# A macaron encoder trunk on one core: three more chunks' down products by seven, a fourth raw buffer, sums into x as two-block views, operands from x times norm weights

## The chip, the cores and the metric

One core of one Trainium2 chip runs the whole program. The time is device microseconds from launch to end. Of the kernel before there are three runs: 2550.9, 2551.19 and 2552.08 us, median 2551.19. One more execution was profiled; its span is 2552.6 us.

In the profile, PE is the matrix engine (PEld its weight loads, which run beside the matmuls), DVE is VectorE, ACT is ScalarE, POOL is GpSimd, and SP is the engine whose queue issues the loads. L12 is line 12 of the kernel.

## What is computed

Two layers, each of a half-step feed-forward block, a mixer (gated short convolution and band attention), and a second half-step feed-forward block; then a final norm. There are 640 token columns (512 of a prompt and 8 x 16 of samples), 1024 channels and 2816 hidden features. All is in float32.

```
def _rmsnorm(x, g):
    xf = x.astype(jnp.float32)
    y = xf * lax.rsqrt(jnp.mean(xf * xf, axis=-1, keepdims=True) + EPS)
    return y.astype(x.dtype) * g

def _swiglu(h, w_gu, w_down):
    gu = h @ w_gu
    g, u = jnp.split(gu, 2, axis=-1)
    return (jax.nn.silu(g) * u) @ w_down

for l in range(DEPTH):
    xp = xp + 0.5 * _swiglu(_rmsnorm(xp, norm_ffn1[l]), w_ffn1_gu[l], w_ffn1_down[l])
    mp, cnp, knp, vnp = _mixer(_rmsnorm(xp, norm_mix[l]), ...)
    xp = xp + mp
    xp = xp + 0.5 * _swiglu(_rmsnorm(xp, norm_ffn2[l]), w_ffn2_gu[l], w_ffn2_down[l])
```

The same runs for the samples, xs. The matter here is the feed-forward blocks, called a0 and b0 in the first layer, a1 and b1 in the second.

## The kernel before

The state x stays in SBUF, transposed: eight tiles x[k] of 128 channels by 640 columns. Columns are halved: t1 is the first 320, t2 the second, and each half of a result has a PSUM bank of its own.

**Precision in three products.** Each float32 operand is split into a high part (a cast on ScalarE, ACT.copy) and a low part (the difference, on VectorE). A product is three matmuls: high by high, high by low, low by high. For weights this is `prep` (L283 and on): the cast whi at L296, and the low split wlo, queued in `pending` and put out by `flush` at L301. Split weights (slabs) have three buffers each.

**Weights.** All weights lie in DRAM as one stream of [128, 1024] blocks in the order of use. `kinds` lists the blocks' kinds; `load` fetches the next block into a raw buffer, of which there are three, through SP's queue. A buffer is free again when the last split of what it held has read it.

**By seven.** Gate and up of one hidden part of 128 features are computed together as a 2 x 2 block product with seven multiplications instead of eight. Two blocks of weights (ra, rb) make four slabs: ra as it is, a sum s65 (two additions at L240, the first of which reads rb), ra after two more additions, and half of rb. `gate_up` runs the seven products, 12 matmuls each, in the order X11, X21, N6, T5, T7, X22, T4, in PSUM banks pa, pb and pc. A product that goes on in pa (N6, T7, T4) follows a read of pa: by ScalarE (c1, u2) or by VectorE (g from pa and c5, before T4).

**Down products.** The 22 hidden parts of a block are cut into chunks (`FFNS`: the chunks' sizes, and how many parts the opening of a0 computes in another way). While the gate and up products of one chunk run, the down products of the chunk before are mixed in. `by_seven` says which chunks have down products by seven as well: chunks of four parts, not those of the opening, and not the last. For those, `Pair` builds the seven operands of two hidden parts (sums on VectorE, a cast on ScalarE, a low split on VectorE, at places that `TURNS` names), and `down_rows` is called twice in the next chunk, after its second and third part (`ROWS`): each call makes four of the eight rows of x. Its seven products, again 12 matmuls each, run in two-bank tiles A and B and two single banks c. What it adds to x is taken from PSUM in three ways: by VectorE directly (`take`, L980), or copied to SBUF by ScalarE (`stage`, L967 and L970) and added by an accumulating DMA that POOL issues (`send`, L975). For other chunks, a down product is one sum over the chunk's parts in a two-bank tile and one update of x on VectorE (L1088).

**Norms.** The norm of the next block is applied after its products: VectorE and ScalarE build operands from x times the norm weights while the last chunk's down products run (`Expand.final`, L516; `norm` for the mixer), and a factor rho per column, found from the sum of squares, multiplies the results. Before the change, the operands of b0, a1 and b1 are multiplied by the previous norm's factor too (`self.prev.rr`), which rho then takes out again (`diagonal`, `inverse`).

**Order.** Within blocks named `manual_schedule(engines=ORDERED)`, PE, VectorE and ScalarE run in the order of the program. From the third part on after the first chunk by seven (`free` in `ffn`) only PE does; the other engines' order is chosen by the scheduler at build time. Every engine executes in order what it was given.

Of the kernel before, what the change touches and what calls it, by code (L numbers as in the profile page):

```python
# [16 lines left out]
P = 128  # L17
# [19 lines left out]
CH = 1024  # L37
# [7 lines left out]
FFNS = {"a0": ((4, 2, 4, 4, 4, 4), 4), "b0": ((2, 4, 4, 4, 8), 0),  # L45
        "a1": ((2, 4, 4, 4, 4, 4), 0), "b1": ((2, 4, 4, 4, 5, 3), 0)}
# [76 lines left out]
def kinds():  # L123


    out = []

    def plain(n):
        out.extend([8] * (n // 8) + [n % 8] * (n % 8 > 0))

    def ffn(name):
        held = 0
        for what, a in ffn_order(name):
            if what == "gu":
                plain(held)
                held = 0
                out.append("gu")
            elif what == "std":
                held += 2 * KT
            elif what == "cut":  # L140
                plain(held)
                held = 0
            elif what == "rows":
                plain(held)
                held = 0
                out.append("gu")
            else:
                held += sum(len(js) for _, js in a)
        plain(held)

    for l in range(L):
        ffn(f"a{l}")
        held = 0
        for what, _ in mixer_order():
            if what == "mix":
                plain(held)
                held = 0
                out.append("mix")
# [16 lines left out]
def trunk(ctx: ExitStack, tc: tile.TileContext, xin, wst, small, pbias, samplebias, kcache, vcache,  # L175
# [43 lines left out]
    slabs, n = [], 0  # L219
    for kind in kinds():  # L220
        if kind in ("gu", "mix"):
            slabs += [(kind, n, i) for i in range(4)]
            n += 2
        else:
            slabs.append(("plain", n, kind * P))
            n += 1
    assert n == wst.shape[0]
# [175 lines left out]
    x = [xp.tile([P, T], F32, name=f"x{k}") for k in range(KT)]  # L403
# [9 lines left out]
    def norm(name, goff, ssum):  # L413
# [18 lines left out]
        st.caps = sp.tile([P, T], F32, tag="rr", name=f"caps{name}", bufs=2)  # L432
        st.rr = sp.tile([P, T], F32, tag="rr", name=f"rr{name}", bufs=2)
# [45 lines left out]
    class Expand(Stats):  # L479
# [4 lines left out]
        def __init__(self, fp, name, goff, prev):  # L484
            super().__init__(name)
            self.fp, self.goff, self.prev = fp, goff, prev
# [3 lines left out]
            self.sq = self.rest = self.rr = None  # L490
            self.known = False

        def final(self, m, square=True):
# [19 lines left out]
            if self.prev is None:  # L513
                DVE.tensor_scalar(out=B, in0=halves(x[m]), scalar1=g, scalar2=None, op0=ALU.mult)
            else:
                DVE.scalar_tensor_tensor(out=B, in0=halves(x[m]), scalar=g, in1=halves(self.prev.rr),  # L516
                                         op0=ALU.mult, op1=ALU.mult)
# [80 lines left out]
        def inverse(self):  # L598

            self.rr = sp.tile([P, T], F32, tag="rr", name=f"rr{self.name}", bufs=2)  # L600
            DVE.tensor_tensor(out=self.rr, in0=self.rho, in1=self.prev.rr, op=ALU.mult)

    def opening(fp, name, goff, n, put, tails):
# [4 lines left out]
        ex = Expand(fp, name, goff, None)  # L608
# [22 lines left out]
        def out(i):  # L631
# [10 lines left out]
            u = tmp(f"u{name}_{j}") if j > 1 else sp.tile([P, T], F32, tag="rr", name=f"u{name}_{j}", bufs=2)  # L642
# [99 lines left out]
    def gate_up(fp, n, ex, first, turned, tails, put, j, pair, later, at):  # L742
# [127 lines left out]
        if first and turned:  # L870
            tails.append(ex.inverse)
# [65 lines left out]
    def down_rows(fp, n, ms, pairs, tails, later):  # L937
# [34 lines left out]

        def send(z, r, cols):
            for u in range(2):
                POOL.dma_start(x[ms[2 * u + r]][:, cols], z[:, u], accum_op=ALU.add)  # L975

        def take(ps, r, cols, scale=0.5):
            for u in range(2):
                xs = x[ms[2 * u + r]][:, cols]
                DVE.scalar_tensor_tensor(out=xs, in0=ps[u], scalar=scale, in1=xs, op0=ALU.mult, op1=ALU.add)  # L980
# [11 lines left out]
        take(b, 0, t1)  # L992
# [11 lines left out]
        send(stage("c7_", A, -0.5), 1, t2)  # L1004
# [9 lines left out]
        take(a, 1, t1, -0.5)  # L1014
        flush()

    def ffn(name, fp, ex, goff, after, end=False):
# [19 lines left out]
        for what, a in ffn_order(name):  # L1037
# [6 lines left out]
            if what == "gu":  # L1044
                turned = after is not None and not end
# [8 lines left out]
                gate_up(fp, f"{name}_{a}", ex, a == plain, turned, tails, act.__setitem__, a, pair, later,  # L1054
# [45 lines left out]
    def mixer(l, after):  # L1100
        with tc.tile_pool(name=f"yp{l}", bufs=1, reuse_waits="tile") as yp, \
# [3 lines left out]
            h, st, stats = norm(f"m{l}", O_GM + l * KT, yas[:, 0, :])  # L1105
# [85 lines left out]
        ex = after(st)  # L1191
# [444 lines left out]
    class Final:  # L1636
# [7 lines left out]
        def all(self, ops):  # L1644
            ws = [[tiles.take() for _ in ops] for m in range(KT)]
            flush()
            rr = sp.tile([P, PARTS[0].stop], F32, tag="rr", name="frr", bufs=2)
# [86 lines left out]
    for l in range(L):  # L1734
# [6 lines left out]
        def after(st):  # L1741
            open_pool(f"fp{l}")
            return Expand(pool[0], f"b{l}", O_G2 + l * KT, st)

        ex = mixer(l, after)
        if l < L - 1:
            ex = ffn(f"b{l}", pool[0], ex, 0,
                     lambda: Expand(pool[0], f"a{l + 1}", O_G1 + (l + 1) * KT, ex))
# [137 lines left out]
```

## Time and profile before

| what | value |
|---|---|
| median of three runs | 2551.19 us |
| span of the profiled execution | 2552.6 us |
| first layer: a0, mixer, b0 | to 440.7, to 853.4, to 1277.8 us |
| second layer: a1, mixer | to 1701.0, to 2113.7 us |
| second layer: b1 and the final norm | to 2552.6 us |
| TensorE's granted clock | 0.998 |
| bytes read from HBM | 225.85 MB |

How to read the profile's lines. A line of waits names the engine, tile and line that waited, after the arrow what ended the wait, and then the total in us, how often, and the longest. A line of the chain in order of time has a start, a duration and what ran; the chain is the work that ended last, followed back from the end. A line of a stretch has its bounds and length, then busy time and number of instructions of PE, PEld, DVE, ACT and POOL, the granted clock, the share of the DMA engines and GB/s. A line of a group has the code line, engine, operation, output and inputs, shapes and count, then busy time in us and the mean of one in ns, and after the second bar the idle time before it and what ended it. Matmuls overlap: one is shown with some 309 ns, but the next of 320 columns starts 147 ns later.

### The profile page before, as it was taken

What the parts mean: (1) busy time and instruction counts of PE and PEld (TensorE: products, weight loads), DVE (VectorE), ACT (ScalarE), POOL (GpSimd) and SP (SyncE); (2) the same over time, 40 slices, a digit from 0 to 9 for tenths busy, and PEclk for the clock granted to TensorE, in tenths of its full rate; (3) what the DMA queues carried; (4) which work ended last, traced back from release to release, by engine and by line L of the source; (5) the groups of instructions that cost most, each with busy time, mean ns of one, the idle gap of its engine ahead of it and who ended that gap; (6) DMA issues with size and microseconds to landing.
All of it is one profiled execution on the core that took longest, in us unless ns stands there. A gap on an engine that the chain in (4) does not pass through costs nothing.

```text
span 2552.6 us, 43143 instructions
## 1 busy us (share of the span) xinstructions
PE 2517.7 (99%) x17264; PEld 2452.2 (96%) x17264; DVE 2095.1 (82%) x3337; ACT 1290.9 (51%) x2036; POOL 243.9 (10%) x361
## 2 busy tenths in 40 slices
PE   8999999999999999999999999999999999999998
PEld 8999999888999999999999999998899999999998
DVE  7788988778677998988799888887786778988875
ACT  5345555665444545555445555556654445455543
POOL 0002111111000002111000122111110000022200
PEclk9999999999999999999999999999999999999999
DMA  3235454335222225443223555443442222255532
GB/s 134 67 102 124 114 127 115 113 104 169 75 85 87 73 96 124 111 117 104 83 83 102 122 124 124 109 109 122 128 136 83 75 91 79 87 124 124 123 101 75
DMA packets 104026, 271.19 MB, mean 106 GB/s; under 512 B 11568, under 2 KB 49072, under 8 KB 103824
## 3 DMA queue, kind: packets, MB, share of 16 engines
q1 hardware_dynamic: 70272, 223.90, 27.2%
q0 software_dynamic: 32832, 43.88, 10.1%
q8 instruction: 135, 2.21, 0.4%
q10 hardware_dynamic: 720, 0.65, 0.1%
q14 instruction: 67, 0.55, 0.1%
HBM read 225.85 MB, written 7.94 MB: 92 GB/s over the span
## 4 chain that ended last, share of the span: by engine, by line
PE 77%; DVE 13%; DMA 4%; ACT 3%; issue 2%; DVEq 0%; ACTq 0%
PE paa L386 10%; PE pab L386 8%; DVE wlo L301 5%; DMA raw<-in_wst 4%; PE py L363 4%; PE pdb L363 4%; PE po L363 4%; PE pda L363 4%; PE pca L386 4%; PE qa L386 4%; PE pcb L386 3%; PE daa L953 3%; PE pba L386 2%; PE pv L1392 2%; PE ma_cv L386 2%; PE dab L953 2%
## 5 line engine op out<-in xcount | busy, mean ns | idle before, releaser
L296 ACT CAST whi<-raw 128x1024 fp32r<-128x1024 f32 (+1 forms) x566 | 506.0, 898 | 390.7 <-PE pca L386 46.5
L301 DVE TENSOR_TENSOR wlo<-raw,whi 128x1024 fp32r<-128x1024 f32 (+1 forms) x566 | 581.5, 1031 | 120.3 <-ACT whi L296 116.6
L296 ACT CAST whi<-s 128x1024 fp32r<-128x1024 f32 (+1 forms) x146 | 137.9, 945 | 245.5 <-DVE s L240 107.6
L386 PE MATMUL pab<-xhib,whi 128*128 128x320 f32 x704 | 220.1, 313 | 9.0 <-DVE gb L240 8.3
L386 PE MATMUL pab<-xlob,whi 128*128 128x320 f32 x704 | 217.3, 309 | 0.0
L386 PE MATMUL pab<-xhib,wlo 128*128 128x320 f32 x704 | 217.3, 309 | 0.0
L386 PE MATMUL paa<-xhia,whi 128*128 128x320 f32 x640 | 199.7, 312 | 8.4 <-DVE ga L240 7.2
L386 PE MATMUL paa<-xloa,whi 128*128 128x320 f32 x640 | 197.5, 309 | 0.0
L386 PE MATMUL paa<-xhia,wlo 128*128 128x320 f32 x640 | 197.5, 309 | 0.0
L301 DVE TENSOR_TENSOR wlo<-s,whi 128x1024 fp32r<-128x1024 f32 (+1 forms) x146 | 158.8, 1088 | 13.8 <-ACT whi L296 13.8
L975 POOL DMA_DIRECT2D x<-c_b x72 | 65.4, 981 | 992.4 <-ACT whi L296 778.4
L240 DVE TENSOR_TENSOR s<-raw 128x512 f32<-128x512 f32 x110 | 75.7, 688 | 94.7 <-DMA raw<-in_wst 94.3
L975 POOL DMA_DIRECT2D x<-c_a x84 | 75.3, 961 | 799.7 <-ACT whi L296 589.6
L386 PEld LDWEIGHTS pab<-xhib,whi 128*128 128x128 f32 x704 | 132.1, 188 | 14.3 <-DVE gb L240 13.0
L386 PEld LDWEIGHTS paa<-xhia,whi 128*128 128x128 f32 x640 | 120.0, 188 | 13.0 <-DVE ga L240 11.6
L386 PEld LDWEIGHTS pab<-xlob,whi 128*128 128x128 f32 x704 | 132.1, 188 | 0.2
L386 PEld LDWEIGHTS pab<-xhib,wlo 128*128 128x128 f32 x704 | 132.1, 188 | 0.0
L386 PEld LDWEIGHTS paa<-xloa,whi 128*128 128x128 f32 x640 | 120.1, 188 | 0.1
L386 PEld LDWEIGHTS paa<-xhia,wlo 128*128 128x128 f32 x640 | 120.1, 188 | 0.0
L386 PE MATMUL pcb<-xhib,whi 128*128 128x320 f32 x352 | 108.6, 309 | 0.0
L386 PE MATMUL pcb<-xlob,whi 128*128 128x320 f32 x352 | 108.6, 309 | 0.0
L386 PE MATMUL pcb<-xhib,wlo 128*128 128x320 f32 x352 | 108.6, 309 | 0.0
(686 smaller groups left out, 7895.1 us busy)
## 6 DMA issues: line engine op xcount, KB each, us to landing
raw<-in_wst SPq DMA_DIRECT2D x384, 512.0 KB, 3.6
x<-c_a POOLq DMA_DIRECT2D x84, 160.0 KB, 4.6
x<-c_b POOLq DMA_DIRECT2D x72, 160.0 KB, 4.3
kc<-in_kcache SPq DMA_DIRECT2D x32, 256.0 KB, 4.2
vc<-in_vcache SPq DMA_DIRECT2D x16, 512.0 KB, 4.5
x<-u_a POOLq DMA_DIRECT2D x28, 160.0 KB, 4.4
bias<-in_pbias POOLq DMA_DIRECT2D x16, 256.0 KB, 3.5
x<-u_b POOLq DMA_DIRECT2D x24, 160.0 KB, 4.4
```

The lines of the kernel that those rows point to most:

```text
L240: DVE.tensor_tensor(out=out, in0=a, in1=b, op=ALU.add)
L296: ACT.copy(hi[:, d], src[:, c])
L301: DVE.tensor_tensor(out=lo, in0=src, in1=hi.bitcast(F32), op=ALU.subtract)
L363: PE.matmul(ps[:, a, :HT], w, x[:, a * HT : (a + 1) * HT], start=first and j == 0, stop=last and j == 2)
L386: PE.matmul(ps, a, b, start=start and kp == 0 and j == 0, stop=stop and kp == NP - 1 and j == 2, skip_group_check=True)
L953: PE.matmul(ps[u], w, y, start=start and i == 0 and j == 0, stop=i == 1 and j == 2, skip_group_check=True)
L975: POOL.dma_start(x[ms[2 * u + r]][:, cols], z[:, u], accum_op=ALU.add)
L1392: PE.matmul(pv[t], xx[:, t * P : (t + 1) * P], w[:, kk * AW : (kk + 1) * AW], start=c == 0 and kk == 0 and j == 0, stop=c == KT // 2 - 1 a ...
```

## The change

- `FFNS`: the chunks of a0 go from 4, 2, 4, 4, 4, 4 to 4, 4, 4, 4, 4, 2, those of a1 from 2, 4, 4, 4, 4, 4 to 4, 4, 4, 4, 4, 2, and those of b1 from 2, 4, 4, 4, 5, 3 to 3, 4, 4, 4, 4, 3. b0 is left as it is. In `ffn_order`, row calls that have no later part to stand behind come after the last part, both in a row.
- Blocks of the stream that belong to a feed-forward block are marked, and every fourth of these is loaded into a buffer of its own, raw4, in the block's pool.
- x is one tile of [128, 8, 640]; x[k] is a view of it. In `down_rows`, `rows` is a view of two blocks of x, two apart. A `send` is one DMA for both instead of one for each; a `take` from A or B is one operation for both. What was staged as c7 and sent is now a take from A on VectorE.
- `Expand.final` multiplies x with the norm weight on ScalarE; the previous norm's factor and what took it out are gone.
- The pool of buffers "rr" is gone: what lay there lies in other pools.

```diff
-FFNS = {"a0": ((4, 2, 4, 4, 4, 4), 4), "b0": ((2, 4, 4, 4, 8), 0),
-        "a1": ((2, 4, 4, 4, 4, 4), 0), "b1": ((2, 4, 4, 4, 5, 3), 0)}
+FFNS = {"a0": ((4, 4, 4, 4, 4, 2), 4), "b0": ((2, 4, 4, 4, 8), 0),
+        "a1": ((4, 4, 4, 4, 4, 2), 0), "b1": ((3, 4, 4, 4, 4, 3), 0)}
@@ def ffn_order(name):
             if ms and by_seven(name, held[0]):
-                if j - j0 in ROWS:
+                while ms and (j - j0 in ROWS or j == j0 + n - 1):
                     out.append(("rows", (ms[:4], held)))
                     ms = ms[4:]
+                    if j < j0 + n - 1:
+                        break
@@ def load(i):
             n = len(raws)
-            raw = wp.tile([P, CH], F32, tag="raw", name=f"raw{n}", bufs=3)
+            if fourth[n] and n % 4 == 3:
+                raw = pool[0].tile([P, CH], F32, tag="raw4", name=f"raw{n}", bufs=1)
+            else:
+                raw = wp.tile([P, CH], F32, tag="raw", name=f"raw{n}", bufs=3)
...
-    x = [xp.tile([P, T], F32, name=f"x{k}") for k in range(KT)]
+    xall = xp.tile([P, KT, T], F32, name="x")
+    x = [xall[:, k] for k in range(KT)]
@@ def final(self, m, square=True):
-            if self.prev is None:
-                DVE.tensor_scalar(out=B, in0=halves(x[m]), scalar1=g, scalar2=None, op0=ALU.mult)
-            else:
-                DVE.scalar_tensor_tensor(out=B, in0=halves(x[m]), scalar=g, in1=halves(self.prev.rr),
-                                         op0=ALU.mult, op1=ALU.mult)
+            ACT.activation(B, halves(x[m]), AF.Copy, scale=g)
@@ def diagonal(self):
             DVE.reciprocal(self.r, self.s)
-            if self.prev is not None:
-                DVE.tensor_tensor(out=self.r, in0=self.r, in1=self.prev.s, op=ALU.mult)
             self.turn(self.ssum, self.r)
...
-        def inverse(self):
-
-            self.rr = sp.tile([P, T], F32, tag="rr", name=f"rr{self.name}", bufs=2)
-            DVE.tensor_tensor(out=self.rr, in0=self.rho, in1=self.prev.rr, op=ALU.mult)
@@ def down_rows(fp, n, ms, pairs, tails, later):
+        def rows(r, cols):
+            return xall[:, ms[r] : ms[r] + 3 : 2, cols]
+
         def send(z, r, cols):
-            for u in range(2):
-                POOL.dma_start(x[ms[2 * u + r]][:, cols], z[:, u], accum_op=ALU.add)
+            POOL.dma_start(rows(r, cols), z, accum_op=ALU.add)

         def take(ps, r, cols, scale=0.5):
-            for u in range(2):
-                xs = x[ms[2 * u + r]][:, cols]
-                DVE.scalar_tensor_tensor(out=xs, in0=ps[u], scalar=scale, in1=xs, op0=ALU.mult, op1=ALU.add)
+            xs = rows(r, cols)
+            for d, z in ((xs, two(ps)),) if ps in (A, B) else zip((xs[:, 0], xs[:, 1]), ps):
+                DVE.scalar_tensor_tensor(out=d, in0=z, scalar=scale, in1=d, op0=ALU.mult, op1=ALU.add)
...
-        take(b, 0, t1)
+        take(B, 0, t1)
...
         mul(a, s2, 0, XT7, False)
-        send(stage("c7_", A, -0.5), 1, t2)
+        take(A, 1, t2, -0.5)
         send(c5, 1, t2)
...
         mul(a, s3, 0, XT4, False)
-        take(a, 1, t1, -0.5)
+        take(A, 1, t1, -0.5)
         flush()
```

More of the change, by code (lines that the diff above doesn't have):

```diff
@@ L123, in kinds, with put @@
 def kinds():
-    out = []
+    out, inside = [], [False]
+    def put(kind):
+        out.append((kind, inside[0]))
     def plain(n):
-        out.extend([8] * (n // 8) + [n % 8] * (n % 8 > 0))
+        for kind in [8] * (n // 8) + [n % 8] * (n % 8 > 0):
+            put(kind)
     def ffn(name):
+        inside[0] = True
         held = 0
@@ L136, in ffn @@
                 held = 0
-                out.append("gu")
+                put("gu")
             elif what == "std":
@@ L145, in ffn @@
                 held = 0
-                out.append("gu")
+                put("gu")
             else:
@@ L157, in kinds @@
                 held = 0
-                out.append("mix")
+                put("mix")
             else:
@@ L214, in split @@
         DVE.tensor_tensor(out=lo, in0=src, in1=hi.bitcast(F32), op=ALU.subtract)
-    slabs, n = [], 0
-    for kind in kinds():
+    slabs, fourth = [], []
+    for kind, inside in kinds():
+        n = len(fourth)
+        fourth += [inside] * (2 if kind in ("gu", "mix") else 1)
         if kind in ("gu", "mix"):
             slabs += [(kind, n, i) for i in range(4)]
-            n += 2
         else:
             slabs.append(("plain", n, kind * P))
-            n += 1
-    assert n == wst.shape[0]
+    assert len(fourth) == wst.shape[0]
     raws, ready = [], []
@@ L740, in seven, with gate_up @@
             last(pa)
-    def gate_up(fp, n, ex, first, turned, tails, put, j, pair, later, at):
+    def gate_up(fp, n, ex, first, tails, put, j, pair, later, at):
         pa, pb, pc = (att(f"p{i}{n}")[:, :HT] for i in "abc")
@@ L1646, in all @@
             flush()
-            rr = sp.tile([P, PARTS[0].stop], F32, tag="rr", name="frr", bufs=2)
+            rr = pool[0].tile([P, PARTS[0].stop], F32, tag="even", name="frr", bufs=1)
             A, B = PARTS
```

32 lines of the change are left out of this document (15 added, 17 removed).

## The prediction

> **What bounds the kernel now.** I read the page first: busy shares and the chain of work that ended last.
>
> ```profile
> span 2552.6 us, 43143 instructions
> PE 2517.7 (99%) x17264; PEld 2452.2 (96%) x17264; DVE 2095.1 (82%) x3337; ACT 1290.9 (51%) x2036; POOL 243.9 (10%) x361
> PE 77%; DVE 13%; DMA 4%; ACT 3%; issue 2%; DVEq 0%; ACTq 0%
> ```
>
> PE is busy for all but 34.9 us, so a matmul taken away is worth its pitch. The chain still runs 20% of the span through VectorE (DVE), DMA and ScalarE (ACT). Next the waits, ending at PE, its weight loads (PEld), VectorE and the load queue.
>
> ```profile
> PE pab L386 <- DVE gb L240: 8.3, 13, 1.7
> PE paa L386 <- DVE ga L240: 7.2, 10, 1.2
> PEld pab L386 <- DVE gb L240: 13.0, 17, 1.9
> PEld paa L386 <- DVE ga L240: 11.6, 15, 1.5
> DVE s L240 <- DMA raw<-in_wst: 94.3, 42, 4.4
> SPq L236 <- DVE wlo L301: 2177.0, 370, 22.4
> ```
>
> The PE waits beyond start and tail are nearly all of one kind: in a gate/up pair, the last product (T4) writes the PSUM bank that VectorE is still adding from (L240, g from pa and c5). The weight loads show 32 such waits, 24.6 us; PE itself shows the 23 longer ones. Why VectorE is late: it stood 94.3 us, 42 times, at the first sum of a weight pair for its load, which had waited for a raw buffer that a low split (L301) still read. One case, in the chain in order of time:
>
> ```profile
> 327.71 5.16 DMA raw<-in_wst
> 332.96 0.09 DVE s L240
> 333.57 1.22 DVE wlo L301
> 334.79 0.41 DVE ga L240
> 335.25 3.79 PE paa L386 x24
> ...
> 346.25 1.22 DVE wlo L301
> 347.46 0.41 DVE ga L240
> 347.92 3.79 PE paa L386 x24
> ```
>
> The load lands at 332.87, then sum, split, the add, then PE. The second case has no load before it: only the split stands ahead of the add, and 24 matmuls take 3.79 us, where 24 take 3.52 undisturbed. Last, the stretches. Four hold the 13 chunks by seven (3, 3, 4 and 3 of them); the fifth is an ordinary chunk.
>
> ```profile
> 198.00:412.00 214.00, 211.77 (x1435) 210.18 (x1434) 184.73 (x284) 112.35 (x162) 42.58 (x49) 1.00 0.52 124
> 937.00:1221.00 284.00, 280.08 (x1897) 278.01 (x1896) 246.64 (x376) 146.74 (x210) 42.25 (x48) 1.00 0.46 114
> 1380.00:1672.00 292.00, 286.52 (x1937) 283.96 (x1937) 251.41 (x388) 152.63 (x220) 56.15 (x64) 1.00 0.51 121
> 2200.00:2458.00 258.00, 253.29 (x1712) 250.95 (x1712) 223.48 (x341) 133.30 (x193) 42.40 (x48) 1.00 0.47 115
> 88.00:198.00 110.00, 109.41 (x744) 108.94 (x743) 85.83 (x127) 43.63 (x63) 0.00 (x0) 1.00 0.28 87
> ...
> 1221.53 56.32 PE pdb L363 x384
> ```
>
> The last row gives the pitch: 56.32 / 384 = 0.1467 us, at a granted clock of 1.00. Counts times pitch are 210.5, 278.3, 284.1 and 251.1 us, so the four stretches lose 3.5 + 5.7 + 7.9 + 6.9 = 24.0 us, the waits' 24.6 again: 1.9 us for each chunk by seven. The ordinary stretch loses 110 - 109.1 = 0.9. VectorE is at 86 to 87% in the four, 78% there.
>
> **The change part by part.**
>
> *Matmuls.* An ordinary chunk of four takes 8 x 4 x 6 = 192 matmuls for its down products, by seven 2 x 84 = 168. The lists give a0 four chunks by seven (before 3), a1 five (4), b1 four (3), b0 three as before. So 72 matmuls go: 72 x 0.1467 = 10.6 us. The changed program's PE order holds 72 fewer. Six weight loads go too, on a queue nobody is short of.
>
> *Fourth raw buffer.* A load now waits for the split four loads back instead of three. In the program's order on VectorE I added up the work, at the durations of the rows, between the split that frees a buffer and the first sum that reads its next load: median 4.4 us before, 10.3 after, and some 5.7 at the least in the steady chunks.
>
> ```profile
> raw<-in_wst SPq DMA_DIRECT2D x384, 512.0 KB, 3.6
> ```
>
> Against 3.6 us to land (5.16 in the case above), the load is there before VectorE asks. Bounds: nothing gained, or all 24.6 us. Nine of the 32 waits are too short for PE's list and are of the second kind, 3.79 - 3.52 = 0.27 us each: 2.4 us that no load causes. They stay, and over 16 chunks instead of 13 become 3.0. Of the other 22.2 I leave a tenth, 2.7 over 16 chunks. Those two remain in place of 24.6: 18.9 us gained. VectorE's cover stays: I sum its work in a steady chunk from 66.2 to 67.5 us, against 6 x 84 x 0.1467 = 73.9 of PE. Without the idle time at loads that fits; with it (94.3 / 13 = 7.3 us a chunk) it did not.
>
> *Sums into x.* Before, a row call made six takes of 128x320, sent eight DMAs and staged c1, u2, c5, c7; now c7 is read by VectorE straight from PSUM, four takes become two of two blocks, a third is the new one, and three DMAs are left.
>
> ```profile
> L1088 DVE SCALAR_TENSOR_TENSOR x<-pdb,x 128x640 f32<-128x640 f32 x32 | 26.2, 820 | 18.6 <-PE pdb L363 18.5
> L980 DVE SCALAR_TENSOR_TENSOR x<-dba,x 128x320 f32<-128x320 f32 x28 | 13.6, 484 | 0.3 <-PE dba L953 0.2
> L967 ACT ACTIVATE c_a<-daa 128x640 f32<-128x640 f32 x28 | 19.6, 702 | 3.8 <-PE daa L953 3.7
> L975 POOL DMA_DIRECT2D x<-c_a x84 | 75.3, 961 | 799.7 <-ACT whi L296 589.6
> ```
>
> VectorE: from 6 x 0.484 = 2.90 us to 3 x 0.820 + 2 x 0.484 = 3.43, 0.5 more a call; ScalarE 0.70 less; POOL issues three DMAs instead of eight, and even at twice 0.96 each it is the freest engine (43 of 214 us). A landing is wanted a chunk later. What matters is the new wait: the fourth use of bank A (T4) now waits for VectorE's take, where it waited for ScalarE's stage. Queued behind that take are the two takes of c, the sums of the next pair and its split, so they are late too; POOL's send of c5 waits for it as well. PE's cover is the product of c between, 12 x 0.1467 = 1.76 us. Two calls of one chunk:
>
> ```profile
> 1130.52 1.23 DVE L301 TENSOR_TENSOR wlo<-raw,whi 128x1024 fp32r<-128x1024 f32 x1 [0.75 <-ACT whi L296]
> 1131.78 0.69 DVE L240 TENSOR_TENSOR raw<-raw,raw 128x512 f32<-128x512 f32 x1
> 1132.86 0.31 PE L953 MATMUL dab<-t4hib,whi 128*128 128x320 f32 x1
> ...
> 1156.28 1.23 DVE L301 TENSOR_TENSOR wlo<-raw,whi 128x1024 fp32r<-128x1024 f32 x1 [0.45 <-ACT whi L296]
> 1157.42 0.48 DVE L980 SCALAR_TENSOR_TENSOR x<-dcb,x 128x320 f32<-128x320 f32 x1
> 1158.00 0.31 PE L953 MATMUL dab<-t4hib,whi 128*128 128x320 f32 x1
> ```
>
> In the changed order the take stands right behind that split. First call: 1131.78 + 0.82 = 1132.60, before PE wants the bank at 1132.86: nothing. Second: 1157.42 + 0.82 = 1158.24 against 1158.00, 0.24 and some 0.1 to start again: 0.35. Over 16 second calls 5.6 us. Bounds: 0, or every one of 32 calls behind one more split, 0.35 + 1.23 = 1.6 us, 51 us. I take 5.6, the case worked out from the place itself.
>
> A rule of the Trainium skill (Perfetto Trace Analysis, Optimizing Scalar/DVE Operations) speaks against this edit: if these engines are not saturated but cause bubbles elsewhere, smaller instructions let work finish sooner. By it the take in two halves would give the first bank 0.4 us earlier, the 5.6 us would not arise, and the sum would be 5.6 lower; no row here shows the halved form at that place.
>
> *Ends of a0 and a1.* The last chunk has two parts instead of four: 96 matmuls of down products before the mixer, 14.1 us instead of 28.2, twice.
>
> ```profile
> 412.00:441.00 29.00, 28.96 (x197) 28.61 (x196) 25.89 (x36) 18.18 (x27) 3.10 (x8) 1.00 0.33 102
> 441.00:454.00 13.00, 13.00 (x59) 10.77 (x58) 13.00 (x21) 7.13 (x11) 0.00 (x0) 1.00 0.33 110
> 454.00:468.00 14.00, 14.00 (x68) 11.60 (x67) 9.57 (x17) 6.66 (x11) 0.00 (x0) 1.00 0.01 2
> 468.00:480.00 12.00, 12.00 (x79) 11.64 (x77) 4.27 (x7) 6.60 (x11) 2.71 (x5) 1.00 0.54 197
> ```
>
> VectorE does 38.9 us in the 42 before the norm's sums (at 454), and has 4.4 + 7.7 = 12.1 us free after. Now 28 us are left before them. Two splits (2.4 us) go; the operands' work can slide into the free 12.1, and the new order does put it there. Nothing, or (38.9 - 2.4 - 28) = 8.5 us twice, 17; I take 1 each, 2 us. The tail of part 21 now runs under the first row call.
>
> *Operands from x times norm weights.*
>
> ```profile
> L516 DVE SCALAR_TENSOR_TENSOR xeb<-x,sm,rrm 128x640 f32<-128x640 f32 x8 | 7.0, 879 | 0.0
> L568 ACT ACTIVATE sqb<-x 128x640 f32<-128x640 f32 x14 | 10.4, 742 | 24.6 <-DVE x L1198 24.6
> ```
>
> 0.88 us leave VectorE for each block, some 0.74 come to ScalarE behind the square. At the last block the chain to PE is up to 0.74 longer; before PE needs it stand 12 + 12 + 9 matmuls, 4.8 us, against about 3.9 us (take 0.82, square, scaling and copy 0.74 each, split 0.82). Nothing; without that cover 3 x 0.74 = 2.2. The dropped norm factors are two small operations each, off the path. One tile for x: the new order shows no wait of one row's sums on another's DMA. Nothing.
>
> *Sum.* 2552.6 - 10.6 - 18.9 + 5.6 + 2.0 = 2530.7 for such an execution. The profiled span lies 1.4 above the median of the runs (2551.19), so 2529.3: I say **2529 us**, 0.9% faster.
>
> **Rivals.**
>
> *The takes hold PE (slower).* In each of 32 row calls PE waits at T4 for the take: 1.6 us as above, 51 in place of 5.6: 2529 + 45 = 2574. For: VectorE is above 86%, in order, and the split ahead waits for ScalarE. Against: the two calls above. It decides from (2551.2 - 2529 + 5.6) / 32 = 0.87 us a call on.
>
> *The loads were hidden anyway: VectorE is the bound.* Freed from loads, it only waits elsewhere and the 24.6 us spread to 16 chunks, 30.3: 2552.6 - 10.6 + 5.7 + 5.6 + 2.0 - 1.4 = 2554: no change. For: the short waits come without a load. Against: 0.27 us each.
>
> *The short ends cost their bound*, 17 instead of 2: 2544. For: VectorE is at 100% at 441 to 454. Against: the idle time behind.
>
> *The fourth buffer does not do what it says*: the loads stand in one queue, every fourth has a buffer of its own, and one that waits holds the next. Half the 22.2 us stay, 13.7 over 16 chunks instead of 2.7: 2540.
>
> **How the numbers follow.** Forecast 62%, takes 10%, VectorE the bound 9%, ends 8%, half a buffer 11%. Low end: no wait left, 2552.6 - 10.6 - 24.6 - 1.4 = 2516. High end: over the ends' case and a little more, 2547; only the cases at 2554 and 2574 lie beyond. 0.2% is 5.1 us, about what a measurement of this kernel tells from no change: faster is below 2546, which the forecast, ends and half-buffer cases give, 81%; of the rest the VectorE case is within, 8%, and 11% slower.
>
> **What will show it.** PE with 72 fewer matmuls at the same pitch; VectorE's wait for raw loads from 94 us to below 20; the waits of weight loads for ga and gb from 24.6 to about 6; a new wait of daa and dab for VectorE's x below 10 us; the norm's sums after a0 without a gap of more than 2 us. Wrong if the ga and gb waits stay above 15 us, or the new wait is above 28.

## The result, and the profile after

| | before | after |
|---|---|---|
| median of the runs, us | 2551.05 (2550.58 to 2552.08, 4 runs) | 2522.69 (2522.14 to 2523.57, 4 runs) |
| profiled span, us | 2552.6 | 2521.0 |
| ratio | | 0.9888, 95% interval 0.9874 to 0.9902 |

28.4 us less by the medians, 31.6 by the profiled spans; forecast were 22, and the time lies inside the range of 2516 to 2547. (The kernel before has one run more here than ahead of the prediction.) The two differences do not agree because the profiled execution of before was a long one: over the runs of all the kernels the time is 1.7 to 2.4 us more than the span of the same execution, for the kernel before 1.7 to 1.8, so its span of 2552.6 belongs to a time of about 2554.4, 3.3 above the median. Some 3 of the 31.6 us are therefore that one execution's and not the change's. The head of the page after, and its chain of work that ended last:

```profile
span 2521.0 us, 42929 instructions
...
PE 2502.0 (99%) x17192; PEld 2441.3 (97%) x17192; DVE 2117.7 (84%) x3347; ACT 1325.1 (53%) x2084; POOL 185.6 (7%) x249
...
PE 92%; ACT 4%; DVE 3%; issue 1%; DMA 0%; DVEq 0%; ACTq 0%
```

72 matmuls fewer, and the chain no longer leaves PE for VectorE and DMA: those held 13% and 4% before, 3% and 0% now. PE is idle 19.0 us instead of 34.9. Next the waits after (us in total, times, longest), with the three rows of VectorE and of the weight loads that answer to those shown of before:

```profile
DVE s L251 <- DMA raw<-in_wst: 2.5, 3, 1.2
...
PEld daa L952 <- DVE x L981: 2.7, 7, 0.4
PEld dab L952 <- DVE x L981: 2.4, 6, 0.4
```

VectorE's 94.3 us at the raw loads are 2.5. Of the waits of PE and its weight loads for ga and gb (24.6 us, 32 times) no row is left at all. The new wait is there, 5.1 us: VectorE's take of bank A ahead of the T4 product, at 13 of the 32 row calls. Two stretches with chunks by seven, in the form in which the four stretches of before were read (us, busy and count of PE and the others, granted clock):

```profile
183.00:400.00 217.00, 216.62 (x1472) 215.68 (x1472) 196.38 (x295) 114.28 (x165) 19.11 (x16) 1.00 0.43 112
...
926.00:1156.00 230.00, 229.61 (x1561) 228.81 (x1561) 206.26 (x308) 118.19 (x169) 21.95 (x18) 1.00 0.44 114
```

Count times 0.1467 us is 215.9 and 229.0: the stretches lose 1.1 and 1.0 us, where before a chunk by seven alone lost 1.9. VectorE is at 90% in them, busier than before.

Where the 31.6 us came from, by the first matmul of each stage (the same boundaries in both traces; the two mixers, each taken alone, repeat to 0.3 us in all traces):

```
stage, from first matmul to first matmul   before    after   change
opening (first poa to first paa)            62.58    61.20    -1.4
a0 (paa to the mixer's pv)                 372.18   364.09    -8.1
b0 (pab to a1's paa)                       424.47   419.56    -4.9
a1 (paa to pv)                             423.13   415.03    -8.1
b1 and its last part (pab to last)         432.33   423.10    -9.2
the two mixers and the rest                837.9    838.0     +0.1
```

### The profile page after: what moved, and what is told of

Same layout as the page of the kernel before. It is cut to its first block, busy times and chain, and to the rows that moved or that the text cites. A ratio compares the mean times of both kernels' runs of the same rounds, so it can differ in the third digit from the quotient of the medians.

```text
span 2521.0 us, 42929 instructions
## 1 busy us (share of the span) xinstructions
PE 2502.0 (99%) x17192; PEld 2441.3 (97%) x17192; DVE 2117.7 (84%) x3347; ACT 1325.1 (53%) x2084; POOL 185.6 (7%) x249
## 4 chain that ended last, share of the span: by engine, by line
PE 92%; ACT 4%; DVE 3%; issue 1%; DMA 0%; DVEq 0%; ACTq 0%
PE pab L397 12%; PE paa L397 11%; PE pcb L397 6%; PE pca L397 6%; PE daa L952 5%; PE py L374 4%; PE po L374 4%; PE qa L397 4%; PE pdb L374 4%; PE dab L952 4%; PE pbb L397 3%; PE pba L397 3%; PE poa L374 2%; PE pda L374 2%; PE pv L1392 2%; PE ma_cv L397 2%
## 5 line engine op out<-in xcount | busy, mean ns | idle before, releaser
L307 ACT CAST whi<-s 128x1024 fp32r<-128x1024 f32 (+1 forms) x152 | 144.4, 950 | 279.5 <-issue 89.3
L312 DVE TENSOR_TENSOR wlo<-s,whi 128x1024 fp32r<-128x1024 f32 (+1 forms) x152 | 166.3, 1094 | 9.8 <-ACT whi L307 9.8
L976 POOL DMA_DIRECT2D x<-c_b x28 | 33.8, 1209 | 1105.6 <-ACT c_b L969 457.8
L976 POOL DMA_DIRECT2D x<-c_a x36 | 43.6, 1212 | 865.1 <-ACT whi L307 386.4
L251 DVE TENSOR_TENSOR raw<-raw,raw 128x512 f32<-128x512 f32 x152 | 103.7, 683 | 0.8
```

The lines of the kernel that those rows point to most:

```text
L251: DVE.tensor_tensor(out=out, in0=a, in1=b, op=ALU.add)
L307: ACT.copy(hi[:, d], src[:, c])
L312: DVE.tensor_tensor(out=lo, in0=src, in1=hi.bitcast(F32), op=ALU.subtract)
L976: POOL.dma_start(rows(r, cols), z, accum_op=ALU.add)
```

## The experiments

Every kernel below is the changed kernel with the edit shown. Spans are of the profiled execution; the ratio is to the kernel before on the same chip, with its 95% interval. The runs of some kernels with three buffers scatter by up to 6.4 us, so where a difference of medians is not that of the spans, it stands beside.

| kernel | span | median | ratio |
|---|---|---|---|
| changed kernel | 2521.0 | 2522.69 | 0.9888 (0.9874 to 0.9902) |
| three raw buffers | 2526.8 | 2527.57 | 0.9900 (0.9883 to 0.9916) |
| chunk sizes of before | 2530.7 | 2532.79 | 0.9922 (0.9907 to 0.9936) |
| c7 staged and sent | 2521.7 | 2524.53 | 0.9890 (0.9875 to 0.9904) |
| blocks scaled by VectorE | 2521.8 | 2523.72 | 0.9886 (0.9871 to 0.9901) |
| three buffers, sums as before | 2550.5 | 2553.75 | 1.0007 (0.9998 to 1.0017) |
| three buffers, c7 staged and sent | 2545.1 | 2549.67 | 0.9987 (0.9978 to 0.9997) |
| three buffers, an extra DMA of 320 KB | 2550.5 | 2555.41 | 1.0007 (0.9997 to 1.0016) |
| three buffers, an extra DMA of 160 KB | 2542.0 | 2543.79 | 0.9965 (0.9952 to 0.9978) |
| sums as before | 2522.9 | 2524.93 | 0.9890 (0.9875 to 0.9905) |
| take of c7 in halves | 2522.1 | 2523.98 | 0.9893 (0.9877 to 0.9910) |
| c7 staged except in the last chunk by seven of a0 and a1 | 2515.2 | 2517.27 | 0.9866 (0.9851 to 0.9881) |
| c7 staged except in that of a0, there the take in halves | 2515.7 | 2517.36 | 0.9866 (0.9851 to 0.9881) |

### Is it the fourth buffer?

```
-            if fourth[n] and n % 4 == 3:
+            if False:
```

> The changed kernel with three raw buffers throughout instead of the fourth inside the FFNs; all else as changed. Theory (late loads made VectorE late for ga and gb, and the fourth buffer is what cured it): VectorE's wait at the weight sums for raw loads goes from 2.5 us back to about 94.3 x 16/13 = 116 us, the waits of PE and its weight loads for ga and gb come back at 24.6 x 16/13 = 30 us, and the time is 2522.7 + 30 = about 2553 us (2547 to 2558). Rival (VectorE has enough slack after the other edits, and the loads were not the cause): loads waited for again, but PE loses under 5 us and the time stays below 2528.

2526.8 us (median 2527.57): the theory fell. VectorE waits for loads again, but PE hardly notices:

```profile
DVE s L251 <- DMA raw<-in_wst: 68.8, 37, 3.5
...
PEld daa L952 <- DVE x L981: 2.7, 7, 0.4
...
PEld pab L397 <- DVE gb L251: 2.4, 4, 0.8
...
PEld paa L397 <- DVE ga L251: 0.4, 1, 0.4
```

With three buffers, as before, and 16 chunks instead of 13, 2.8 us of waits for ga and gb are left. So in the changed kernel the fourth buffer is worth 5.8 us by the spans and 4.9 by the medians; something else in the change had cured the rest. The rows of the two traces say what to look for. Of VectorE's waits for a load, 25 in the kernel before are longer than 1.5 us; their loads landed 5.1 us after issue on average, with 3.4 DMAs of the sums into x (160 KB each) in flight at some time beside them. With three buffers and the new sums there are 27 such waits, but the loads landed after 3.5 us, with 1.1 sum DMAs (320 KB each) beside them. Averaged over a load's time, 1.65 sum DMAs were in flight in the first case and 0.35 in the second. (Counted over both traces, issue, landing and wait of each load.)

### The sums into x, with three buffers and with four

The sums as before, once with three raw buffers and once with four:

```
-            POOL.dma_start(rows(r, cols), z, accum_op=ALU.add)
+            for u in range(2):
+                POOL.dma_start(x[ms[2 * u + r]][:, cols], z[:, u], accum_op=ALU.add)
...
-        take(A, 1, t2, -0.5)
+        send(stage("c7_", A, -0.5), 1, t2)
```

(and the takes of one block each). With three buffers:

> The changed kernel with three raw buffers and with the sums into x as before (eight DMAs of one block, six takes of one block, c7 staged); the chunk sizes and the operands' edit stay. With three buffers and the new sums the time was 2527.6 us (profiled 2526.8), with only 2.4 us of weight load waits left for gb. New theory (most of the 24.6 us of waits for ga and gb were caused by the sums' DMAs, which lie in the way of the weight loads; the waited-for loads of the kernel before land 5.1 us after issue with 3 to 5 such DMAs in flight, 3.3 us in the kernel with three buffers and the new sums): the waits come back at 24.6 x 16/13 = 30 us, those of daa and dab (6.2) go, and the time is 2527 + 30 - 3 - 6 = about 2548 us (2542 to 2553). Rival (the operands' edit or the chunk sizes cured them): under 6 us of ga and gb waits, 2522 to 2528 us.

2550.5 us (median 2553.75). VectorE's wait for loads and the waits for ga and gb are back:

```profile
DVE s L251 <- DMA raw<-in_wst: 102.2, 34, 4.7
...
PEld paa L397 <- DVE ga L251: 15.0, 19, 1.5
PEld pab L397 <- DVE gb L251: 12.5, 17, 1.6
PEld pda L374 <- DVE x L1089: 6.6, 1, 6.6
```

27.5 us for ga and gb, 30 expected; the loads behind the 27 long waits land after 5.1 us again. (The last row is another matter, below.) With four:

> The changed kernel with the fourth raw buffer, and the sums into x as before. Theory (either cure is enough: a load that is four splits ahead lands in time even past the DMAs): ga and gb waits below 6 us, the daa and dab waits of 5.1 us gone, so 2517 to 2524 us, the stall of 5 us at the end of a0 as with c7 staged counted in the upper end. Rival (the fourth buffer alone does not cover the slower loads): 6 to 20 us of ga and gb waits remain and the time is 2526 to 2540.

2522.9 us, with no wait for ga or gb, as this view of VectorE's and PE's waits shows:

```profile
DVE s L251 <- DMA raw<-in_wst: 2.9, 4, 1.1
...
PE pda L374 <- DVE x L1089: 5.2, 1, 5.2
```

The four spans side by side:

```
                       sums as changed    sums as before
four raw buffers            2521.0             2522.9
three raw buffers           2526.8             2550.5
```

Either edit alone takes away nearly all of the waits: the fourth buffer 27.6 us where the sums are as before, the new sums 23.7 us where there are three buffers. After the first of them the other has 2 to 6 us left to gain. (By the medians it is 28.8 and 26.2, then 2.2 and 4.9.) Both figures of the right column hold one thing more: PE's wait at pda, the last row of both views, 6.3 us by PE's own rows with three buffers and 5.2 with four. It has nothing to do with ga and gb, and is taken up with the staging of c7 below; without it the sums as before would not be the slower form with four buffers.

### Which part of the sums

c7 staged and sent, the two-block views kept, three buffers:

> The changed kernel with three raw buffers and with c7 staged by ScalarE and sent by DMA (four DMAs of two blocks a call, none for the third take); the two-block views stay. Theory (bytes of sum DMAs next to the load decide): a third more of them than with three buffers alone, so the load that VectorE waits for lands some 0.6 us later, a fair part of the ga and gb waits is back (8 to 20 us), and daa and dab waits go (-6): 2529 to 2541 us, between the kernel with three buffers (2527.6) and the one with all sums as before. Rival (the number and form of DMAs counts, eight against four, not the bytes): ga and gb waits stay below 5 us and the time is about 2522 plus the a0 stall of 5 us that the staged form had with four buffers, 2522 to 2528.

2545.1 us (median 2549.67), past the upper end. 20.1 us of the ga and gb waits are back (11.6 and 8.5, in the view of the weight loads), and the waited-for loads land after 4.5 us. The kernel before sent 8 x 160 = 1280 KB in a row call, this one 4 x 320 = 1280, the changed one 3 x 320 = 960. The two-block form of sends and takes, with the same bytes sent, is worth 5.4 us (2550.5 - 2545.1; 4.1 by the medians), c7's 320 KB and its staging 18.3 (2545.1 - 2526.8), with a stall at pda of 5.4 in it, of the kind that is shown below.

Is it the traffic, or the order in which VectorE and ScalarE now work? The next kernel leaves both engines' work alone; it adds a DMA, and for GpSimd the zeroing of the tile that this DMA adds into:

```
         take(A, 1, t2, -0.5)
+        spare = fp.tile([P, 2, HT], F32, tag="spare", name=f"spare{n}", bufs=1)
+        POOL.memset(spare, 0.0)
+        POOL.dma_start(spare, u2, accum_op=ALU.add)
         send(c5, 1, t2)
```

> The changed kernel with three raw buffers, and in every row call one more accumulating DMA of two blocks (320 KB) from u2 into a tile that nothing reads, issued by GpSimd ahead of c5's; nothing else is added but the zeroing of that tile by GpSimd, so VectorE, ScalarE and PE do the same work as with three buffers alone (2527.6 us). Theory (the sum DMAs delay the weight loads): VectorE's wait for raw loads rises from 68.8 us to 90 or more, the loads that it waits for land at 4 us or more instead of 3.3 to 3.6, ga and gb waits rise by 5 us or more and the time is 2533 to 2543 us. Rival (the order of VectorE's and ScalarE's work made the difference, not the traffic): within 3 us of 2527.6.

2550.5 us (median 2555.41), 23.7 more than without it and over the theory's upper end; the rival is out. One row call, first without the extra DMA (three buffers): GpSimd's issues, the load's, VectorE's sum that waits for it and the add to ga that PE needs.

```profile
205.45 1.20 POOL L976 DMA_DIRECT2D x<-c_a  x1 [4.85 <-DVE x L981]
206.18 1.70 POOL L976 DMA_DIRECT2D x<-u_a  x1
...
211.23 1.32 SPq L247 DMA_DIRECT2D raw<-in_wst  x2
...
214.53 0.69 DVE L251 TENSOR_TENSOR s<-raw 128x512 f32<-128x512 f32 x1 [2.33 <-DMA raw<-in_wst]
215.14 1.22 DVE L312 TENSOR_TENSOR wlo<-raw,whi 128x1024 fp32r<-128x1024 f32 x1
216.28 0.48 DVE L251 TENSOR_TENSOR ga<-paa,c_a 128x320 f32<-128x320 f32 x1
```

And with it:

```profile
201.50 1.02 POOL L1008 DMA_DIRECT2D sparea<-u_a  x1
207.45 0.64 POOL L1007 MEMSET sparea<- 128x640 f32 x1 [4.93 <-DMA sparea<-u_a]
208.09 1.20 POOL L976 DMA_DIRECT2D x<-c_a  x1
208.80 1.73 POOL L976 DMA_DIRECT2D x<-u_a  x1
...
211.87 1.36 SPq L247 DMA_DIRECT2D raw<-in_wst  x2
...
216.49 0.69 DVE L251 TENSOR_TENSOR s<-raw 128x512 f32<-128x512 f32 x1 [3.65 <-DMA raw<-in_wst]
217.10 1.22 DVE L312 TENSOR_TENSOR wlo<-raw,whi 128x1024 fp32r<-128x1024 f32 x1
218.24 0.48 DVE L251 TENSOR_TENSOR ga<-paa,c_a 128x320 f32<-128x320 f32 x1
```

The load is issued 0.6 us later but VectorE gets it 2.0 later: from its issue to VectorE's sum it takes 3.3 us without and 4.6 with the extra DMA. The extra DMA itself is long over by then (GpSimd's next zeroing of its tile waits 4.93 us for it to land); what lies beside the load are the call's own sums, which stand behind that zeroing in GpSimd's queue and go out 2.6 us later. So it is for all 27 loads behind the long waits: no extra DMA is in flight beside any of them, while 2.0 of the calls' own sums are, on average, instead of 1.1, and the loads land after 4.9 us instead of 3.5. The 23.7 us are therefore not the price of 320 KB of traffic as such: the zeroing, which waits for the extra DMA, pushes the sums into the load. That the sums' DMAs make the load late is what the run shows. What the DMA engines do from 204 to 216 us, around that call, is in the view of transfers (queue: packets, MB, share of the 16 engines), without the extra one:

```profile
q0 software_dynamic: 574, 0.68, 37.6%
q1 hardware_dynamic: 284, 1.05, 26.9%
```

GpSimd's sums (software queue) take 37.6% for 0.68 MB, the loads 26.9% for 1.05: a megabyte of sums takes 55.3 of these per cent against 25.6, 2.2 times as much, by the time of the packets. The packets are 1.2 KB against 3.7.

Half of the extra bytes:

> The kernel with three raw buffers and an extra DMA in every row call, with half the bytes (one block, 160 KB, instead of 320 KB); three buffers alone: profiled 2526.8, with the whole extra DMA 2550.5. Theory (the load's landing moves by what lies in the way, and PE waits as soon as the sum's slack is used up): landing of the waited-for loads between 3.5 and 4.9 us, time between, nearer to the lower end as the slack covers the first part: 2530 to 2540. Rival (one more DMA costs by its presence, whatever its size): 2547 or more.

2542.0 us (median 2543.79), 2 over the expected range: the first 160 KB cost 15.2 us, the next 8.5. By the ratios, which set each run against the kernel before on its own chip, it is some 17 and 11 us; with 2 to 4 us of uncertainty either way on each ratio, whether the cost is out of proportion is not shown. The loads behind the long waits land after 3.5, 4.4 and 4.9 us without, with half and with the whole extra DMA. Here too no extra DMA lies beside these loads: it is the calls' own sums that come later.

### The rest of the change

The chunk sizes of before:

```
-FFNS = {"a0": ((4, 4, 4, 4, 4, 2), 4), "b0": ((2, 4, 4, 4, 8), 0),
-        "a1": ((4, 4, 4, 4, 4, 2), 0), "b1": ((3, 4, 4, 4, 4, 3), 0)}
+FFNS = {"a0": ((4, 2, 4, 4, 4, 4), 4), "b0": ((2, 4, 4, 4, 8), 0),
+        "a1": ((2, 4, 4, 4, 4, 4), 0), "b1": ((2, 4, 4, 4, 5, 3), 0)}
```

> The changed kernel with the chunk sizes of the kernel before (13 chunks by seven instead of 16); all else as changed. Theory (a chunk by seven is worth its 24 matmuls of 0.1467 us, less 0.4 us of waits in its row calls, and the short ends cost nothing): 72 matmuls come back, +10.6, of the 5.1 us of row call waits about 1 goes, so 2522.7 + 9.6 = about 2532 us (2530 to 2535); the 1.4 us that the opening gained stay if they are from the operands' edit. Rival (the short last chunks of a0 and a1 cost the 8 us each that the last stretch might): then the time comes out at 2526 or below. Rival (the new chunk sizes also took away waits at the ends): above 2537.

2532.79 us: 10.1 more, as the theory had it, and 9.7 by the spans. By stages the new sizes give 4.5 us in a0, 1.7 in a1 and 3.7 in b1. a1 falls 1.8 us short of its 24 matmuls (3.5 us). 1.3 of these are waits of PE for ScalarE at its start, with a first chunk of four, which the changed kernel's list of PE's waits shows and the one with the old sizes does not:

```profile
PE paa L397 <- ACT c_a L833: 0.6, 1, 0.6
PE pca L397 <- ACT c_a L836: 0.4, 2, 0.2
...
PE paa L397 <- ACT c_a L820: 0.3, 1, 0.3
```

Operand blocks scaled by VectorE:

```
-            ACT.activation(B, halves(x[m]), AF.Copy, scale=g)
+            DVE.tensor_scalar(out=B, in0=halves(x[m]), scalar1=g, scalar2=None, op0=ALU.mult)
```

> The changed kernel with the operand block x times norm weight made by VectorE (tensor_scalar) instead of ScalarE, in all four expansions; the form without the norm factors stays. Theory (the waits of PE for ScalarE's c_a and xhi at the start of a1, about 2.0 us of lost pitch, come from the 32 activations moved to ScalarE): they vanish, and VectorE's 0.7 us more a block costs PE nothing there: 2520.5 us (2519 to 2522). The opening's 1.4 us also go back if ScalarE's help made them (then about 2522). Rival (VectorE is at 84% and the blocks stand ahead of its splits): new waits for VectorE at the start of b0, a1 and b1 cost 3 us or more and the time is above 2525.

2521.8 us. The waits at a1's start stayed, so they do not come from the scaling. In the opening two waits of the kernel before are back, which the changed kernel lacks:

```profile
PE poa L374 <- DVE ua L489: 0.9, 1, 0.9
...
PE paa L397 <- ACT c_a L767: 0.5, 1, 0.5
```

ScalarE's scaling gains these 1.4 us in the opening and loses 0.3 to 0.5 in each of b0, a1 and b1. (The opening's length alone says less: among the kernels with the changed form of that part it runs from 61.05 to 62.50 us. It is the two waits that tell, which none of those has.)

c7 staged and sent again, with four buffers (the line of c7 alone undone):

> The changed kernel with c7 of every row call staged by ScalarE and sent by DMA, as before, instead of VectorE's sum straight from PSUM; the other edits of the sums stay. Theory (the 5.1 us of weight load waits of daa and dab at T4 are for VectorE's take, which stands behind a low split): these waits vanish at all 13 places, each worth 0.3 to 0.4 us, and the time is 2517.5 us (2516 to 2520). Rival (ScalarE's staging and one more DMA a call only move the wait: ScalarE's split and its sums are 0.7 us later, twice in 16 chunks): waits of paa, pab or daa for ScalarE of 4 us or more appear and the time is 2521 to 2526.

2521.7 us, over the theory's 2516 to 2520; the time is the rival's, but not its reason, for PE got no new waits for ScalarE. It has two parts. All 13 waits of daa and dab are gone: b0, a1 and b1 are 1.3, 1.7 and 1.7 us shorter. a0 is 5.5 longer, at one place, shown in the chain of this kernel in order of time:

```profile
413.32 5.75 DMA x<-c_a
419.07 0.40 issue
419.47 5.67 DMA x<-c_a
...
425.22 0.07 ACT ya L438
...
428.70 0.83 DVE x L1088
429.53 0.04 issue
429.57 2.50 PE pda L374 x8
```

The sums of c7 and c5 by DMA go to the same x blocks one after the other, 5.7 us each; the mixer's norm needs the sum, ScalarE stands at ya for it, VectorE behind ScalarE and PE behind VectorE: 5.1 us. It is the row of pda in every kernel above with the new chunk sizes and c7 sent in a0's last chunk by seven.

So c7 by VectorE only there, staged elsewhere:

```
-        take(A, 1, t2, -0.5)
+        if n[:5] not in ("a0_16", "a1_16"):
+            send(stage("c7_", A, -0.5), 1, t2)
+        else:
+            take(A, 1, t2, -0.5)
```

> The changed kernel, four raw buffers, with c7 staged by ScalarE and sent by DMA as before except in the row calls of the last chunk by seven of a0 and of a1, ahead of the mixer, where VectorE takes it. Theory (staging frees PE of the waits of daa and dab, and its only price with four buffers was the stall of 5.1 us at the end of a0, where ScalarE waits for the last sum DMA): 2521.7 - 5.1 - some 0.5 of order, profiled span about 2516.5 (2515.5 to 2518). Rival (the stall comes from the earlier calls' DMAs too): it stays and the span is 2520 to 2522.

2515.2 us, 0.3 below the range, no wait of daa or dab, no stall: 5.8 us below the changed kernel by the spans, 5.4 by the medians.

The take in halves, which the Trainium skill's rule on breaking up instructions ("Perfetto Trace Analysis", Optimizing Scalar/DVE Operations) had suggested:

```
-            for d, z in ((xs, two(ps)),) if ps in (A, B) else zip((xs[:, 0], xs[:, 1]), ps):
+            for d, z in ((xs, two(ps)),) if whole and ps in (A, B) else zip((xs[:, 0], xs[:, 1]), [ps[:, u, :HT] for u in range(2)] if ps in (A, B) else ps):
...
-        take(A, 1, t2, -0.5)
+        take(A, 1, t2, -0.5, False)
```

> The changed kernel with VectorE's take of c7 in two halves of 128x320, all else as changed. Theory (PE's T4 product waits for the first half of bank A alone, 0.4 us earlier, which is the rule of the Trainium skill on smaller instructions): the 13 waits of daa and dab, 5.1 us, vanish; VectorE does 0.15 us more a call; profiled span 2516 to 2517. Rival (the bank is freed as a whole, or the second half comes too late): waits of 0.3 us or more remain at the 13 places and the span is 2520 to 2523.

2522.1 us; the rival's. The same place in the changed kernel's and in this kernel's VectorE:

```profile
1067.41 1.23 DVE L312 TENSOR_TENSOR wlo<-raw,whi 128x1024 fp32r<-128x1024 f32 x1 [0.45 <-ACT whi L307]
1068.55 0.82 DVE L981 SCALAR_TENSOR_TENSOR x<-dab,x 128x640 f32<-128x640 f32 x1
```

```profile
1067.98 1.22 DVE L312 TENSOR_TENSOR wlo<-raw,whi 128x1024 fp32r<-128x1024 f32 x1 [0.45 <-ACT whi L307]
1069.12 0.88 DVE L981 SCALAR_TENSOR_TENSOR x<-dab,x 128x320 f32<-128x320 f32 x2
```

PE's T4 product starts at 1069.42 and at 1070.05, each time 0.05 us after the end of the whole take (1069.37; 1069.12 + 0.88 = 1070.00), not of its first half at about 1069.6. Halves end 0.06 us later than the whole and help nobody. The reason is in the program as built: in the trace the first half raises no semaphore, in any of the 32 calls, and only the second does; PE's first T4 matmul waits for that one. So PE was never told of the first half. Two tiles instead of one for the two banks, each with a signal of its own, were not tried, and what the smaller pieces would then give is not shown.

Both together, the staged form, in a1's last chunk by seven too, and halves in that of a0:

> The two above together: c7 staged and sent everywhere except in a0's last chunk by seven, where VectorE takes it in halves. Theory: no wait of daa or dab at all and no stall: profiled span 2515.5 to 2517, the fastest of all. Rival (a1's end stalls as a0's did): 2520 or more.

2515.7 us, as the one before within what can be told; a1's end does not stall.

The fourth buffer in the kernel before itself was not tried (the nearest is the kernel with four buffers and the sums as before): it takes the room that the norm factors' tiles leave.

## Why the prediction was right, and where it was not

*Matmuls, right.* 10.6 us forecast; the chunk sizes are worth 9.7 by the spans, 10.1 by the medians, with the waits that they bring.

*The fourth raw buffer: right in the mechanism's first half, wrong in whose doing it was, and too small.* The prediction said that VectorE is late for ga and gb because its load is late, and the load because of the buffer. The runs with three buffers bear that out: where the waited-for loads take 4.4 us or more the waits are there (14.0 to 27.5 us), at 3.5 us hardly any (2.8). But a load was late for two reasons at once, its buffer and the sums in its way, and the step "a landing is wanted a chunk later", which looked only at when the sums' own landing is needed, passed over what they do to others. The row was there: the case shown in the chain landed after 5.16 us, where the view of issues gave 3.6 as the median. The forecast treated that as scatter. So the sum credited the buffer with 18.9 us; the waits it wanted to remove were 24.6, all went, and in the changed kernel the buffer's own part is 5.8. The new sums, priced at a loss of 5.6 us, alone gain 23.7 with three buffers. With the sums as before the buffer does alone what was forecast of it, and more: no wait for ga or gb, 27.6 us. The forecast's total came out near because either edit was enough for these waits and it had counted on one of them. That it did not see the other cure cost it nothing, since the first had already taken the waits; this is luck.

The rival of "half a buffer", by which a load that waits for its buffer holds up the next, did not come: with four buffers VectorE waits 2.5 to 2.9 us for its loads, whichever form the sums have.

The short waits of 0.27 us "that no load causes" were to stay and be 3.0 us; none is left. They show as waits of about 0.35 us of the weight loads (8 before), and return with late loads and the old sums together (12 between 0.3 and 0.36 us in the kernel with both undone). With four buffers and the old sums there are none, and with late loads and the new sums hardly any: of 25 waits one is below 0.4 us with the whole extra DMA, of 15 three with the half. So a late load is a condition for them after all; how they come of the two is not shown.

*Sums into x: the wait right, its remedy wrong.* Waits of 5.1 us against 5.6, 13 places instead of 16, worked out from the right place: VectorE's take behind a low split. Staging c7 where that is free of the stall shows what they cost: 5.8 us. The sentence on the rule of the Trainium skill, by which halves would remove them, did not come true: PE waited for the whole take, since the first half signals nothing. The rule itself is not refuted by that.

*Short ends of a0 and a1, 2 us forecast, none seen.* The mixer's first part (from its first pv to its first qk matmul) takes 29.49 us before and after. But this holds because c7 no longer goes by DMA: with c7 sent, the short end costs 5.1 us in a0, since the sums of the last row call then land next to the norm. So an end can cost what lies within the bound of 8.5 us a piece, but by a landing, not by VectorE's work as the bound had it.

*Operands, nothing forecast.* A gain of 1.4 us in the opening, by the two waits there, and a loss of about 1 later. The prediction looked for the price at the last block only and not at the opening, where PE waited for VectorE.

*Not foreseen:* PE's wait for ScalarE at a1's start, 1.3 us in the rows above, from the new first chunk.

*The other rivals.* Takes that hold PE at all 32 calls did not come: 0.4 us at 13 of them, far from the 0.87 a call at which that case decides. Nor is VectorE the bound: it is at 90% in the stretches and PE loses 1 us in 217.

Against the forecast sum, in us of the spans: waits for ga and gb 5.7 more gained, ends 2.0, opening 1.4, the row calls 0.5, a1's start 1.3 lost; 8.3 together, of the 9.7 between 2530.7 and 2521.0. The rest was not assigned to a step. By the medians the forecast is 6.6 us off (2529.3 against 2522.7): the 2530.7 was for an execution as long as the profiled one of before, and some 3 of the 9.7 us are that. In which of the rows above they lie is not shown, so the account is not closed to better than that.

## What to carry to other kernels

When a load is late, ask two questions of the same row: when could it be issued, and how long did it take against its median; the second names the traffic beside it, which a transfer that "nobody waits for" still is. Two edits that cure the same wait must not be added up: undo each alone and both together, for each on its own looked worthless here (1.9 and 5.8 us) while the pair is worth 29.5. The first of these also hid a loss and a gain of 5 us each, which only the undoing of c7 alone took apart. A sum moved from a DMA to a compute engine has two prices, the engine's time and the DMA's way, and best is often a mix by place: here DMA in the steady chunks, VectorE where the sum is read next.

## What the runs showed of the hardware

A weight load of 512 KB that VectorE waits for takes 3.5 us on average with one sum DMA of 320 KB beside it, mostly for a short while, and 5.1 with three or four of 160 KB, though it is issued on another queue. The Trainium skill ("DMA: Bandwidth & Descriptors", Issuing engines are not separate DMA queues) says that transfers started by different engines run on the same 16 DMA engines and interleave; the traces agree, 3.3 against 4.6 us in the two row calls shown. What the runs add is the size: in the 12 us looked at, the packets of accumulating DMAs within the on-chip memory take 2.2 times as much of the DMA engines' time a megabyte as those of the loads. And the moment counts: sums that go out 2.6 us later, into a load, are enough to lengthen it by 1.3 us, though no byte more lies beside it than the call's own. Whether the size of the packets (1.2 KB against 3.7) or the addition makes it dear, no run here tells.
